# Bias rows and mask products in place of bias tables, scan products on four array quadrants, and three engines in written order

## The chip, the cores and the metric

The kernel runs on one core of one Trainium2 chip. The metric is the device time of one execution in microseconds; less is better. The profile gives busy times of TensorE (PE, and PEld for its weight loads), VectorE (DVE), ScalarE (ACT), GpSimd (POOL) and the queue of SyncE (SP), which issues all the DMAs of this program.

## The reference, cut to what matters

One layer over 2048 latent tokens (a grid of 32 rows by 64 columns) with 256 context tokens ahead of them. One input projection feeds two branches: neighbourhood attention and a gated delta rule in both directions; both are gated, projected, merged and projected again.

```python
# neighbourhood attention, per grid row r: 8 rows x 16 columns of keys around each query, plus all context keys
s_win = einsum('bqhd,bywhd->bhqyw', q_r, k_band) + bias      # bias: learned, by row and column distance
s_win = where(col_in, s_win, -inf)                           # only the query's own 16 columns
s_ctx = einsum('bqhd,bchd->bhqc', q_r, kc)
pr = softmax(concatenate([s_win, s_ctx]))                    # one softmax over both
o_na = pr_win @ v_band + pr_ctx @ vc
# delta rule, per chunk of 64 tokens and direction, state S (64 x 64 per head)
v_new = u_i - w_i @ S
o_i = qd_i @ S + qk_i @ v_new
S = S * gt_i + kd_i.T @ v_new
# merge
y = sigmoid(g_na) * ((o_na * silu(z_na)) @ w_o_na) + sigmoid(g_dn) * ((rmsnorm(o_dn) * silu(z_dn)) @ w_o_dn)
out = x + gate * (y @ w_out)
```

## The kernel before

All matrix products that need more than one pass of reduced precision are written as three products of a high and a low part (names ending in H and L, or `hi` and `lo`); the small ones of the scan, of the transposes and of the values run in plain float32, which TensorE takes in two passes.

The stages, in order of time. **Setup** (0 to 126 us): norms and transposes of the inputs. **Delta-rule projections**: the blocks for q, k and v with short convolution, then `kk_tile`, which forms the k k^T and q k^T products of each chunk, beside gate projections. **Attention projections** (`na_pair`, 920 to 1271 us): 52 tiles of 256 tokens in six series (v, k, v, k, q, q), each tile 48 matmuls on L729; tiles of k and q are normalised: squares on ACT (L691), a scale on DVE (L693), a power on POOL (L694), a multiplication on ACT (L697), then, two tiles later, a transpose on PE (L707), an eviction on ACT into the single buffer `nhi` (L710) and a store. DVE runs the triangular solves (`solve`, L580 and L582) beside it. **Bias tables** (`table_load`, `table`, L760 to L787): for each of the 8 heads, 8 DMAs bring skewed rows of the padded bias from `d_rp` into `trr` (16 partitions each), and 9 additions on POOL (L782) add them to masks read from `k_mk`; the results go to `d_tab`. The scheduler places this work beside the later attention projections and the gate projections, from 1091 us on. **Last gate units and the scan over the context** (1393 to 1451 us).

**Attention and scan** (1451 to 2009 us). A loop of 32 units: 2 groups of 4 heads (`hg`), 4 groups of 8 grid rows (`rg`), 4 groups of 16 columns (`cg`). A unit has 128 queries and a band of 12, 15 or 16 rows by 24 or 32 columns of keys, so 288 to 512 window keys, and 256 context keys. It treats its 4 heads as two pairs `pr`. For each pair: `scores` (three products for each head on L1079, then one DVE operation, L1089, that adds the bias table and takes the row maximum), `scores_ctx` (the same against context keys, L1079; the maximum on L1096, its negative `nm` on L1098, and four exponentials on ACT, L1101 and L1104), `turn` (transposes of the window probabilities, L1112, copied by DVE and ACT, L1114), `turn_ctx` (L1121, L1123), `values` (L1132, L1136), and for the unit `sums_inv` (L1140 to L1144) and `finish` (L1149 to L1153). The queries of two units come by one DMA and are split by `split_later` into `qh` (ACT, L977) and `ql` (POOL, L978). The tables come from `d_tab`: those of the inner row groups into `tmid`, the others into `tedge`.

Between these calls, `pump(chain, n)` advances the scan, one step of both directions for each unit: `times_state` twice (L882: k and q against the state, DVE on L884 and L887), `cT` (L898), its copy `cw` on ACT (L900), `ckd` (L905, state update on L906), `cA` (L912, output `co` on L914), and on POOL the state's decay (L894) and, in the second half, the sum of the two directions (L892). Direction 0 lies on partitions 0 to 63, direction 1 on 64 to 127; each product is 64 x 64 on the quadrant of the array where its rows and columns have the same half. From unit 17 on a unit also holds `dn_out` of the step before: a square on ACT (L928), its sum on DVE (L930, L931), a power on POOL (L933), a multiplication on DVE (L934), four transposes on PE (L938), one DVE operation (L939) and a store.

PE runs the loop in the order in which it is written (`manual_schedule` on L994); the order on DVE, ACT, POOL and SP is that of the program's scheduler, which goes by its own costs. Every engine then executes its own list strictly in that order. **Output** (2009 to 2389 us): the branch projections (L1356) and the final one (L1367).

## Time and profile before

| | us |
|---|---|
| device time, median of 3 runs | 2390.23 (2381.87 to 2395.80) |
| profiled execution, its own time | 2390.53 |
| span from its first to its last instruction | 2388.7 |
| PE busy / DVE / ACT / POOL | 2198.5 / 1500.3 / 849.5 / 943.1 |

Busy times are shares of the whole span; how much an engine is waited for differs by stage, so the sections below go by stretches of time. A matmul's end is modelled, so PE reads as busy a little beyond its last column. The granted clock of TensorE is shown as a share of 2.4 GHz; its mean was 0.973.

### The profile page before, as it was taken

To read this page: it belongs to the slowest core of one execution; us is meant where nothing else is said; L and a number is where in the kernel's file an instruction comes from. 1 tells how busy PE (TensorE), PEld (TensorE's weight loads), DVE (VectorE), ACT (ScalarE), POOL (GpSimd) and SP (SyncE) were. 2 spreads that over 40 slices of the span, in tenths; PEclk is the share of its full clock that TensorE was granted. 3 is DMA by queue.
4 is the path that set the end of the run, shared out by engine and by line. 5 is a ranking of instruction groups with operands and counts; after the bars stand their busy time and mean duration, and the time that the engine had idled before them with its cause. 6 is when DMAs were issued, how large, how long until landed. Compare 5 with 4: busy or idle time off the path is not lost. (4 is left out here: it accounts for less than half of the span.)

```text
span 2388.7 us, 47331 instructions
## 1 busy us (share of the span) xinstructions
PE 2198.5 (92%) x18359; PEld 1842.5 (77%) x18359; DVE 1500.3 (63%) x2410; ACT 849.5 (36%) x2624; POOL 943.1 (39%) x784
## 2 busy tenths in 40 slices
PE   6999999998989999999889997999888988999999
PEld 2778777876767778998887876777666766889988
DVE  3736877469959969859669813666566766222222
ACT  4524344344333332434554112444334444211110
POOL 2514777654423102316758410211133325543442
PEclk8999999999999999999999998999999999999999
DMA  7323444665574153254676667877877776444342
GB/s 267 105 74 76 115 126 121 158 154 141 146 190 124 55 127 89 60 135 132 179 189 187 167 182 214 224 188 205 210 200 186 186 194 195 139 118 128 108 116 91
DMA packets 461592, 358.17 MB, mean 150 GB/s; under 512 B 203253, under 2 KB 386697, under 8 KB 460809
## 3 DMA queue, kind: packets, MB, share of 16 engines
q1 hardware_dynamic: 461368, 355.16, 55.6%
q8 instruction: 144, 2.36, 0.4%
q14 instruction: 80, 0.66, 0.1%
HBM read 231.71 MB, written 119.67 MB: 147 GB/s over the span
## 5 line engine op out<-in xcount | busy, mean ns | idle before, releaser
L179 PE MATMUL pd<-hT,slots 128*128 128x512 f32 (+1 forms) x3360 | 812.5, 396 | 1.8 <-ACT hT L319 1.7
L179 PEld LDWEIGHTS pd<-hT,slots 128*128 128x128 f32 x3360 | 619.0, 191 | 146.8 <-issue 3.8
L580 DVE TENSOR_TENSOR tmp<-Xs 128x236 f32<-128x236 f32 (+43 forms) x310 | 313.0, 1010 | 38.3 <-DMA Xs<-d_X 26.1
L582 DVE TENSOR_TENSOR Xs<-Xs,tmp 128x236 f32<-128x236 f32 (+43 forms) x310 | 324.2, 1046 | 8.6
L125 POOL TENSOR_TENSOR slots<-w_raw,slots 128x512 fp32r<-128x512 f32 (+1 forms) x76 | 117.3, 1544 | 343.2 <-ACT slots L124 336.5
L729 PE MATMUL pd<-slots,hT 128*128 128x256 f32 x1248 | 162.2, 290 | 0.0
L729 PE MATMUL pd<-wide,hT 128*128 128x256 f32 x1248 | 159.5, 290 | 2.4 <-ACT wide L124 1.3
L729 PEld LDWEIGHTS pd<-wide,hT 128*128 128x128 f32 x1248 | 156.4, 197 | 3.2 <-ACT wide L124 1.8
L729 PEld LDWEIGHTS pd<-slots,hT 128*128 128x128 f32 x1248 | 156.9, 193 | 0.0
L1101 ACT ACTIVATE pr<-pr,nm 128x288 f32<-128x288 f32 (+3 forms) x128 | 77.9, 609 | 161.3 <-DVE nm L1098 161.3
L894 POOL TENSOR_TENSOR sd<-sd,gts 128x512 f32<-128x512 f32 x36 | 37.6, 1043 | 214.2 <-PE pc L882 200.2
L1357 DVE SCALAR_TENSOR_TENSOR gt<-gt,pu 128x256 f32<-128x256 f32 x120 | 46.2, 418 | 120.4 <-DMA gt<-d_g 62.5
L782 POOL TENSOR_TENSOR tmk<-trr,tmk 128x288 f32<-128x288 f32 (+3 forms) x72 | 99.4, 1397 | 37.9 <-DMA tmk<-in_k_mk_dram 33.2
L484 DVE SCALAR_TENSOR_TENSOR y<-raw,vT,y 128x512 f32<-128x512 f32 (+1 forms) x112 | 95.1, 860 | 24.3 <-ACT raw L472 20.4
L1371 DVE SCALAR_TENSOR_TENSOR ckd<-pf,gate 128x512 f32<-128x512 f32 x32 | 22.0, 691 | 122.2 <-PE pf L1367 111.7
L1356 PE MATMUL pu<-ckq,OS 128*128 128x256 f32 x512 | 95.2, 284 | 1.5 <-DVE gt L1357 1.4
L205 ACT ACTIVATE zt<-pd 128x512 f32<-128x512 f32 x73 | 43.3, 593 | 145.9 <-PE pd L179 80.2
L694 POOL TENSOR_TENSOR nrn<-nss,nhalf 128x8 f32<-128x8 f32 x34 | 72.6, 2136 | 54.6 <-DVE nss L693 54.3
L1358 POOL TENSOR_TENSOR gt<-gt 128x256 f32<-128x256 f32 x60 | 44.1, 735 | 123.8 <-DVE gt L1357 111.5
L124 ACT CAST slots<-w_raw 128x512 fp32r<-128x512 f32 (+1 forms) x76 | 46.6, 613 | 129.9 <-DMA w_raw<-in_w_in_dram 107.7
L1359 ACT CAST yh<-gt 128x256 fp32r<-128x256 f32 x60 | 24.3, 406 | 187.4 <-POOL gt L1358 187.3
L1112 PE MATMUL pt<-ident,pr 128*128 128x128 f32 (+2 forms) x416 | 66.2, 286 | 23.5 <-ACT pr L1101 22.3
(298 smaller groups left out, 4614.8 us busy)
## 6 DMA issues: line engine op xcount, KB each, us to landing
w_raw<-in_w_in_dram SPq DMA_DIRECT2D x92, 256.0 KB
ckq<-d_kq SPq DMA_DIRECT2D x64, 256.0 KB
gt<-d_g SPq DMA_DIRECT2D x60, 256.0 KB
d_g<-zt SPq DMA_DIRECT2D x41, 256.0 KB
d_X<-X SPq DMA_DIRECT2D x72, 128.0 KB
Xs<-d_X SPq DMA_DIRECT2D x18, 512.0 KB
cv<-d_v SPq DMA_DIRECT2D x72, 128.0 KB
cT<-d_T SPq DMA_DIRECT2D x72, 128.0 KB
```

What stands on the lines that cost most here:

```text
L124: S.copy(hi[:, j:j + 4, 0:n], wr)
L125: G.tensor_tensor(out=lo[:, j:j + 4, 0:n], in0=wr, in1=hi[:, j:j + 4, 0:n].bitcast(F32), op=ALU.subtract)
L179: PE.matmul(ps[0:n, 0:m], a[:, k, 0:n], h_part(g, z, k), start=k == 0 and i == 0, stop=k == KB - 1 and i == 2)
L484: V.scalar_tensor_tensor(out=y[:, 0:m], in0=raw[:, o + j - 1:o + j - 1 + m], scalar=tap(j), in1=y[:, 0:m], op0=ALU.mult, op1=ALU.add)
L580: V.tensor_tensor(out=tv, in0=X[r, piv, cols].unsqueeze(1).to_broadcast([8 * n, m, w]), in1=X[r, rows, piv].unsqueeze(2).to_broadcast([8 * ...
L582: V.tensor_tensor(out=X[r, rows, cols], in0=X[r, rows, cols], in1=tv, op=ALU.add)
L694: G.tensor_tensor(out=rn, in0=ss, in1=nhalf, op=ALU.pow)
L729: PE.matmul(ps[:, 256 * i:256 * i + 256], h[:, 256 * j + P * i:256 * j + P * i + P], w[:, :, part, k, :], start=k == 0 and n == 0, stop=k ...
L782: G.tensor_tensor(out=mv, in0=rr[:, k0:k0 + nr, w0:w0 + n], in1=mv, op=ALU.add)
L1101: S.activation(e[:, 0:nk], e[:, 0:nk], AF.Exp, bias=nm[:, u:u + 1], accum_out=self.sums[:, hh, 0:1])
L1112: PE.transpose(ptw[0:kb, b, :], self.et[u][:, kb * b:kb * b + kb], ident)
L1356: PE.matmul(ps, a, r[:, k, :], start=k == 0 and n == 0, stop=k == 3 and n == 2)
```

## The change

It has three parts.

1. **Bias and masks.** The tables, their DMAs and their POOL additions are gone. `load_bias` brings the skewed bias rows of 4 heads straight into an SBUF tile `bias` (two of them), with the same 8 DMAs for each head; for the first group all 32 are issued ahead of the first query load, for the second group four in each of units 6 to 13. The mask is added on PE: two more products for each head and pair in `scores`, ahead of the three others and into the same PSUM region, with a 64-row one-hot matrix of the query's row (then of its column) as stationary operand and a row (column) mask, repeated by a stride of zero, as moving one. DVE then adds the bias from a strided view of the tile.
2. **Scan.** `times_state` becomes one block: for each head, the products with k and with q follow each other, the latter into the other half of the partitions, so four quadrants take part. In the same way `ckd` and `cA` are interleaved. Buffers in DRAM that hold tokens of the scan's output swap halves, and a second copy of the decay factors with halves swapped (`egw`) is loaded.
3. **Order.** DVE, ACT and POOL too run the 32 units in the order in which they are written, and that order is changed: five advances of the scan for each unit in place of seven, `scores_ctx` ahead of `values`, both `turn_ctx` copies on ACT, `dn_out` spread over the second, third and fourth advance, `sums_inv` after the second `turn`.

```diff
-    def table(h):
-        ...
-                SP.dma_start(out=mk, in_=k_mk[:, ty, o:o + nr * n])
-                ...
-                G.tensor_tensor(out=mv, in0=rr[:, k0:k0 + nr, w0:w0 + n], in1=mv, op=ALU.add)
-                SP.dma_start(out=d_tab[:, ty, h, o:o + nr * n], in_=mk)
...
-            def times_state(z):
-                ps = pc.tile([P, H, C], F32, name="pc")
-                for h in range(H):
+            pss = [pc.tile([P, H, C], F32, name="pc") for _ in range(2 if main else 1)]
+            for h in range(H):
+                for z, ps in enumerate(pss):
                     for d in range(2):
-                        PE.matmul(ps[half[d], h, :], ld["ckq"][half[d], ho(h), z, :], sd[half[d], h, :], start=True, stop=True)
+                        PE.matmul(ps[half[d ^ z], h, :], ld["ckq"][half[d], ho(h), z, :], sd[half[d], h, :], start=True, stop=True)
...
             for h in range(H):
                 for d in range(2):
                     PE.matmul(p4[half[d], h, :], ld["ckd"][half[d], h, :], w[half[d], h, :], start=True, stop=True)
+                for d in range(2 if main else 0):
+                    PE.matmul(p3[half[1 - d], h, :], ld["cA"][half[d], ho(h), :], w[half[d], h, :], start=True, stop=True)
...
+        def load_bias(hg):
+            z = ap.tile([P, 4, 16, 47], F32, name="bias", bufs=2)
+            for h in range(4):
+                for qr in range(8):
+                    if qr % 4 == 0:
+                        yield z
+                    o = ((4 * hg + h) * 23 + 7 - qr) * 47
+                    behind(SP.dma_start(out=z[16 * qr:16 * qr + 16, h].rearrange("q k w -> q (k w)"), in_=skew[:, o:o + 16 * 47]))
...
+                for i, (a, b) in enumerate(more):
+                    for u, r in enumerate(halves):
+                        PE.matmul(out(u), a[r], b[r], start=i == 0, stop=False)
...
-                    V.tensor_tensor_reduce(self.e[u][:, 0:nk], pws[u][:, 0:nk], self.tab[pr][:, u, 0:nk], 1.0, -3.0e38, ALU.add, ALU.max, self.mx[:, u, 0:1])
+                    V.tensor_tensor_reduce(rc(self.e[u][:, 0:nk]), rc(pws[u][:, 0:nk]), biases[self.hg][:, 2 * pr + u, k0:k0 + self.nr, w0:w0 + w], 1.0, -3.0e38, ALU.add, ALU.max, self.mx[:, u, 0:1])
...
-        mid_load = load_mid(0)
-        mids = {0: next(mid_load)}
+        bias_load = load_bias(0)
+        biases = {0: next(bias_load)}
+        for _ in bias_load:
+            pass
+        mkraw = ap_("fwr").rearrange("p a b -> p (a b)")[:, 0:432]
+        SP.dma_start(out=mkraw, in_=k_mk)
...
         load_q(0)()
...
+        order_all = tc.manual_schedule(engines={mybir.EngineType.DVE, mybir.EngineType.Activation, mybir.EngineType.Pool})
+        order_all.__enter__()
```

The loop's body after the change (the diff of it is long):

```python
pump(chain, 1); un.turn(); un.scores(1)
pump(chain, 1); un.turn_ctx(); un.scores_ctx(1)
pump(chain, 1); un.values(0)
pump(chain, 1); splits; un.turn(); un.sums_inv(); nu.scores(0)      # nu: the next unit
pump(chain, 1); un.turn_ctx(); nu.scores_ctx(0); un.values(1); un.finish()
```

**SP, just ahead of the first unit.** `fwr<-d_nq` is the load of the first queries, `tmid` a table, `d_g<-zd` the store of the last gate unit. Before:

```order
L863 DMA cv<-d_v 64x512
L864 DMA cT<-d_T 64x512
L863 DMA cv<-d_v 64x512
L864 DMA cT<-d_T 64x512
L974 DMA fwr<-d_nq 128x2x256
L992 DMA tmid<-d_tab 128x1232
L211 DMA d_g<-zd 128x512
```

and now, with line numbers of the changed program (`bias<-d_rp` is one of the 32 loads of bias rows):

```order
L834 DMA cv<-d_v 64x512
L835 DMA cT<-d_T 64x512
L975 DMA bias<-d_rp 16x752 x2
L213 DMA d_g<-zd 128x512
L975 DMA bias<-d_rp 16x752 x30
L1221 DMA fwr<-in_k_mk_dram 128x432
L951 DMA fwr<-d_nq 128x2x256
```

The first query load has moved behind 32 loads of bias rows, the masks and a store.

**PE, a unit with `dn_out`** (15-row band, 360 keys), from the last transposes of the unit before on. Before:

```order
L1149 MATMUL po<-ident,rb 128x128 x2
L882 MATMUL pc<-sd,ckq 64x64 x16
L1112 MATMUL pt<-ident,pr 120x128 x6
L882 MATMUL pc<-sd,ckq 64x64 x16
L1121 MATMUL pt<-ident,pr 128x128 x4
L1079 MATMUL pw<-KH,qh 128x360 x2
L1079 MATMUL pw<-KL,qh 128x360 x2
L1079 MATMUL pw<-KH,ql 128x360 x2
L898 MATMUL pc<-cv,cT 64x64 x16
```

and now (`mkr` are the mask products, L913 the transposes of `dn_out`):

```order
L853 MATMUL pc<-sd,ckq 64x64 x32
L1091 MATMUL pt<-ident,pr 120x128 x6
L1051 MATMUL pw<-mkr 128x360 x4
L1054 MATMUL pw<-KH,qh 128x360 x2
L1054 MATMUL pw<-KL,qh 128x360 x2
L1054 MATMUL pw<-KH,ql 128x360 x2
L1100 MATMUL pt<-ident,pr 128x128 x4
L1054 MATMUL pw<-KHc,qh 128x256 x2
L1054 MATMUL pw<-KLc,qh 128x256 x2
L1054 MATMUL pw<-KHc,ql 128x256 x2
L871 MATMUL pc<-cv,cT 64x64 x16
L1111 MATMUL po<-pT,vt 64x128 x6
```

The two blocks of 16 scan products have become one of 32, four mask products stand ahead of the scores, and the context transposes and scores now stand ahead of `cT`.

**DVE, the same kind of unit**, where `dn_out` has its sum (`so`) and its multiplication (`co<-co,ro`). Before, at the unit's end:

```order
L1089 ISA mx 128x1
L930 TENSOR_REDUCE so<-ob 128x8
L931 TENSOR_SCALAR so<-so 128x8
L1096 TENSOR_REDUCE mx<-pw 128x1 x2
L1152 TENSOR_TENSOR azt<-po,azt 128x16x16
L1098 TENSOR_REDUCE nm<-mx 128x2
L1153 TENSOR_TENSOR azt<-po,azt 128x16x16
L934 TENSOR_TENSOR co<-co,ro 128x512
```

and now, in mid-unit (`pr,mx<-pw,bias` is the addition of the bias):

```order
L857 TENSOR_TENSOR cr<-pc,egw 128x512
L1075 TENSOR_REDUCE mx<-pw 128x1 x2
L1077 TENSOR_REDUCE nm<-mx 128x2
L905 TENSOR_REDUCE so<-ob 128x8
L906 TENSOR_SCALAR so<-so 128x8
L909 TENSOR_TENSOR co<-co,ro 128x512
L914 SCALAR_TENSOR_TENSOR zd<-pc,vT,zd 128x512
L1093 COPY pT<-pt 128x384
L1119 TENSOR_TENSOR ri<-sums 128x4
```

The multiplication by `ro`, which POOL makes from `so`, follows `so` directly, and the copy `pT` of the second `turn` stands behind both it and `zd`.

## Rows read from the trace of the kernel before

**Rows 1.** Windows by stage: length, busy time and instructions by engine, clock, DMA.

```profile
1091.00:1290.00 199.00, 172.41 (x1299) 165.37 (x1298) 150.71 (x157) 107.13 (x629) 143.97 (x90) 0.95 0.67 178
1451.00:1480.80 29.80, 17.01 (x257) 13.91 (x257) 10.32 (x30) 6.83 (x21) 2.71 (x3) 0.77 0.79 208
1480.80:1744.40 263.60, 235.81 (x3986) 189.34 (x3984) 167.44 (x449) 112.74 (x339) 47.38 (x52) 0.97 0.80 208
1744.40:2008.60 264.20, 232.09 (x3791) 184.99 (x3790) 186.26 (x470) 118.79 (x339) 91.89 (x87) 0.97 0.73 190
```

**Rows 2.** Windows, of L729 alone: length, PE and PEld busy, clock, DMA.

```profile
992.20:1035.10 42.90, 42.90 (x338) 41.54 (x337) 1.00 0.59 125
1101.60:1265.00 163.40, 136.82 (x1011) 131.69 (x1010) 0.95 0.69 183
```

**Rows 3.** Chain of waits from 1091 to 1290 us: total, times, longest.

```profile
ACT nx L697 <- POOL nrn L694: 51.1, 21, 4.2
ACT nhi L710 <- DMA d_nq<-nhi: 14.5, 5, 6.1
```

**Rows 4.** Groups by line, POOL, 1091 to 1290 us: busy, mean ns, idle before.

```profile
L782 POOL TENSOR_TENSOR tmk<-trr,tmk 128x288 f32<-128x288 f32 (+3 forms) x51 | 68.7, 1366 | 23.3 <-DMA tmk<-in_k_mk_dram 19.3 <-issue 1.9 <-DMA d_nk<-nhi 1.8
```

**Rows 5.** Timeline of SP around 1154 us: start, duration, four issues merged.

```profile
1153.76 1.81 SPq L768 DMA_DIRECT2D trr<-d_rp  x4
```

**Rows 6.** Timeline ahead of the first unit: start, duration, idle time before in brackets.

```profile
1455.43 0.37 SPq L974 DMA_DIRECT2D fwr<-d_nq  x1
...
1461.59 0.62 ACT L977 CAST qh<-fwr 128x512 fp32r<-128x512 f32 x1 [11.28 <-DMA fwr<-d_nq]
...
1462.26 0.61 PE L1079 MATMUL pw<-KH,qh 64*128 64x288 f32 x2 [11.51 <-ACT qh L977]
```

**Rows 7.** Timeline of PE within one unit.

```profile
1645.06 1.15 PE L882 MATMUL pc<-sd,ckq 64*64 64x64 f32 x32
...
1647.78 1.15 PE L882 MATMUL pc<-sd,ckq 64*64 64x64 f32 x32
1648.86 0.66 PE L1121 MATMUL pt<-ident,pr 128*128 128x128 f32 x4
...
1649.72 0.32 PE L1079 MATMUL pw<-KL,qh 64*128 64x360 f32 x2
1649.88 0.33 PE L1079 MATMUL pw<-KH,ql 64*128 64x360 f32 x2
```

**Rows 8.** Windows of 0.20 us in one `kk_tile`, L628 alone (passes under way).

```profile
626.95:627.15 0.20, 0.20 (x8) 0.16 (x4) 1.00 0.26 62
626.40:626.60 0.20, 0.20 (x16) 0.20 (x10) 1.00 1.15 267
```

**Rows 9.** Windows: unit 12, and unit 17.

```profile
1659.90:1674.00 14.10, 13.65 (x249) 11.11 (x247) 10.13 (x28) 6.11 (x20) 1.44 (x2) 1.00 0.87 233
1744.40:1767.60 23.20, 17.90 (x252) 14.28 (x251) 12.49 (x32) 7.99 (x23) 5.77 (x6) 0.85 0.85 206
```

**Rows 10.** Chain of waits, 1480 to 2009 us.

```profile
DVE pr L1089 <- DMA tedge<-d_tab: 17.2, 8, 4.4
...
PE pw L1079 <- POOL ql L978: 11.6, 11, 2.0
...
PE pw L1079 <- DVE mx L1089: 10.2, 8, 3.6
```

**Rows 11.** Groups by line, DVE, ACT and POOL, 1760 to 2011 us.

```profile
L1096 DVE TENSOR_REDUCE mx<-pw 128x1 f32<-128x256 f32 x56 | 21.1, 418 | 8.8 <-PE pw L1079 8.5
L884 DVE TENSOR_TENSOR cr<-pc,egs 128x512 f32<-128x512 f32 x28 | 19.2, 687 | 8.7 <-PE pc L882 8.3
L1089 DVE CUSTOM_DVE_ANT_0 pr<-pw,tmid 128x360 f32<-128x360 f32 (+1 forms) x32 | 18.4, 608 | 4.5 <-PE pw L1079 4.5
L1114 DVE COPY pT<-pt 120x384 f32<-120x384 f32 (+3 forms) x29 | 17.0, 586 | 0.8 <-PE pt L1112 0.8
...
L1101 ACT ACTIVATE pr<-pr,nm 128x360 f32<-128x360 f32 (+3 forms) x57 | 35.0, 615 | 63.5 <-DVE nm L1098 63.5
L1104 ACT ACTIVATE pr<-pw,nm 128x256 f32<-128x256 f32 x58 | 26.3, 455 | 0.0
...
L933 POOL TENSOR_TENSOR ro<-so,nh 128x8 f32<-128x8 f32 x15 | 24.7, 1647 | 30.9 <-DVE so L931 30.6
L892 POOL TENSOR_TENSOR cr<-cr,OS 128x512 f32<-128x512 f32 x14 | 18.7, 1337 | 0.0
L894 POOL TENSOR_TENSOR sd<-sd,gts 128x512 f32<-128x512 f32 x14 | 14.6, 1043 | 54.9 <-PE pc L882 52.5 <-DMA ckd<-d_kd 2.5
L978 POOL TENSOR_TENSOR ql<-fwr,qh 128x512 fp32r<-128x512 f32 x7 | 8.9, 1270 | 0.0
```

More of the change, by code (lines that the diff above doesn't have):

```diff
@@ L956, in scan @@
                 yield
-                yield from step
-                yield
+                next(step, None)
                 yield
@@ L1071, in __init__, with products @@
                 self.po = None
-            def products(self, pr, keys, out):
+            def products(self, pr, keys, out, more=()):
                 q0 = P * (self.n % 2)
+                halves = [slice(64 * u, 64 * u + 64) for u in range(2)]
+                for i, (a, b) in enumerate(more):
+                    for u, r in enumerate(halves):
+                        PE.matmul(out(u), a[r], b[r], start=i == 0, stop=False)
                 for i, (a, b) in enumerate(((0, 0), (0, 1), (1, 0))):
-                    for u in range(2):
-                        r = slice(64 * u, 64 * u + 64)
-                        PE.matmul(out(u), self.qs[a][r, pr, q0:q0 + P], keys(b)[r], start=i == 0, stop=i == 2)
+                    for u, r in enumerate(halves):
+                        PE.matmul(out(u), self.qs[a][r, pr, q0:q0 + P], keys(b)[r], start=i == 0 and not more, stop=i == 2)
             def scores(self, pr):
@@ L1280, in body @@
             un.turn()
-            nu = Unit(n + 1, *ahead) if ahead else None
-            pump(chain, 1)
-            un.turn_ctx(1)
+            un.sums_inv()
+            nu = Unit(n + 1, ahead) if n < 31 else None
             if nu:
@@ L1287, in body @@
                 pump(gprod, 1000)
-            un.values(1)
+            pump(chain, 1)
+            un.turn_ctx()
             if nu:
                 nu.scores_ctx(0)
+            un.values(1)
             un.finish()
-            pump(chain, 1)
             un = nu
```

141 lines of the change are left out of this document (57 added, 84 removed).

## The prediction

> **What bounds the kernel now.** I first cut the span into stages by windows of busy time, then asked in each which wait ends last. Three stages hold everything that the change touches: the stretch in which the bias tables are made, the start of the attention, and the 32 units.
>
> In 1091 to 1290 us PE is busy for 172.4 of 199.0 us, with the DMA engines at 0.67 and the clock at 0.95 [rows 1]. Seven tiles of L729 without table work beside them took 42.9 us, 6.13 each; 21 tiles with it took 163.4 us, 7.78 each [rows 2]. So the stretch is 21 x 1.65 = 34.7 us longer than at the earlier pace. The chain of waits says where: ACT's normalising multiplication waits 51.1 us in all for POOL's `nrn`, and its eviction 14.5 us for the store that empties `nhi` [rows 3]. POOL meanwhile makes 51 table additions of 1.37 us [rows 4], and `nrn` queues behind them. Behind it, beside the gate units, PE is busy for 102.1 of 103.0 us [rows 1]: no room, nothing to win.
>
> At the start of the attention PE stands idle for 11.5 us, since the first queries' load was issued at 1455.43 and `qh` could be made only at 1461.59 [rows 6]. The stretch ran at clock 0.77 [rows 1].
>
> In the units PE is the bound: 235.8 of 263.6 us in the first half, 232.1 of 264.2 in the second, while DVE has 167 and 186, POOL 113 and 119 [rows 1]. What PE lacks goes to single waits: `ql` from POOL, 11.6 us, and the maximum of DVE, 10.2 us, which itself waits 17.2 us for table loads [rows 10]. Two units show the spread: unit 12 takes 14.1 us, 13.65 of it PE work; unit 17, the first with `dn_out`, 23.2 us at clock 0.85 with one wait for DVE's maximum of up to 3.6 us [rows 9, 10].
>
> **The tables.** With the POOL additions and their DMAs gone, POOL has `nrn` as its first duty again. All of the 34.7 us would return if the tables were the whole difference, none if these series (queries, with stores to `nhi` [rows 3]) were slower by themselves. The 14.5 us behind `nhi`'s stores need not be the tables' doing, but the table DMAs share their queue. I take three quarters, **-26**, bounds 0 and -35.
>
> **The start.** Thirty of the 32 bias loads, the masks and the last gate store now stand ahead of the first query load. Four such loads took 1.81 us on SP [rows 5], so 30 take 13.6, and the mask load one more of 0.4; two table loads at about 0.5 each go. All of it stands on the path: PE has nothing before the queries come [rows 6]. **+13**; bounds 0 (if SP gets to these loads well before) and +16 (all 32, the masks and the store's own time).
>
> **PE's work in a unit.** Removed: a block of 16 scan products is 32 passes in 1.15 us [rows 7], of which about 0.2 is the modelled tail, so 0.94. What a block takes with four quadrants is read from `kk_tile`, where windows of equal length hold 8 passes with two quadrants in use and 16 with four, at full clock in both [rows 8]: a pass costs its quadrant 0.05 us (0.20 x 2 / 8 and 0.20 x 4 / 16) either way. Two blocks of 32 passes become one that lasts as long as either, and this happens twice in a unit: 2 x 0.94 = -1.88. Added: mask products. Two products over 360 keys (both heads of a pair, on opposite row halves) start 0.16 us apart [rows 7]; there are two such steps in a `scores` call and two calls: 4 x 0.16 = +0.66. A moving operand with a stride of zero isn't in the trace; were it twice as slow, another 0.66 x 32 = 21 us would go, and at no cost at all 21 come back. I take it as an ordinary one, since only its address is special. Net -1.2 a unit, -39 over 32, if waits stayed as they are.
>
> The Trainium skill speaks against the four quadrants: its page "TensorEngine Tiling (Array Packing)", section "Restrictions and Gotchas", says that different row tiles can't access the same PSUM bank at the same time. By it the four would run two at a time, and the saving of 60 us (32 x 1.88) would be nil. The trace disagrees: L882 writes both row halves into one buffer, and its 32 passes took 1.15 us where one after the other they would need 32 x 0.05 = 1.6 [rows 7, 8].
>
> **Waits in a unit.** The order on the other engines is now written, so I walked one unit by hand, from the end of the block of 32. PE needs 0.8 (second `turn`), 1.0 (scores with masks), 0.55 (`turn_ctx`, L1121's 0.66 less its tail [rows 7]), 0.6 (context scores), 1.0 (`cT`) and 1.45 (values): 5.4 to the next `turn`. DVE needs in its order `cr` and `cv` 0.69 each, `pT` 0.58, two bias operations of 0.61, `cr` again, two maxima of 0.42, `nm` 0.15: 4.9 with the operations' accumulator reads; then ACT's exponential 0.61 and its sum 0.19 [rows 11]: 5.9. So `turn` waits about 0.5; `cw`, behind four exponentials, costs 0.1. Unit 12's 13.65 [rows 9] becomes 13.65 - 1.88 + 0.66 = 12.4; with the waits **13.0** for an even unit. In an odd unit the split of the next queries stands in the written order behind `cw`: `qh` 0.61 on ACT [rows 6], then `ql` 1.27 on POOL [rows 11], and the next unit's scores wait some 2.2: **15.1**. Six of the key splits (1.27 on POOL [rows 11]) in the first 16 units add 7.6, and four units with 512 keys about 1 each. Units 1 to 16: 8 x 13.0 + 8 x 15.1 + 7.6 + 4 = 236 against 263.6 [rows 1]: **-27**. The table loads' waits on DVE (17.2 [rows 10]) are in that difference.
>
> From unit 17 on `dn_out` comes in. Four transposes add 0.55 to PE. Its chain is: DVE done with `nm` at 5.1, `so` 0.68 and its scaling 0.27 on DVE, POOL busy with the sum of directions (1.34) and the decay (1.04) until 6.6, `ro` 1.65 [rows 11], so 8.25, `co` 0.69, so 8.95. PE, in its written order, stands at the transposes at 5.4: it waits 3.55, in place of the 0.5 above. 12.95 + 3.55 = **16.5**; 15 x 16.5 + 4 = 251.5 against 264.2: -13. Such waits lower the clock: unit 17 lost (1 - 0.85) x 23.2 = 3.5 us beside a wait of 3.6 [rows 9, 10]. I take half of that in about a quarter of the 15 units, +6 (bounds 0 and 52): **-7**. Queued behind `co` on DVE are `zd` and the copy `pT` of the next `turn`, so the wait is late for `values` too, but PE has stood still meanwhile.
>
> Queue of SP: by the changed program's order about 19 DMAs a unit, at 0.45 [rows 5] are 9 us, with four bias loads 11, less than a unit. It hides behind PE, and would cost only if units fell below that.
>
> **Sum.** 2390.5 - 26 + 13 - 27 - 7 = **2343 us**, against the profiled execution's 2390.53 (span 2388.7 and 1.8 around it), which stands 0.3 above the median of the runs, 2390.23.
>
> **Rivals.**
> 1. *The `dn_out` wait costs more.* For it: every wait of 3.5 us is as long as unit 17's [rows 10]. Against it: in the second half as a whole the clock was 0.97 [rows 1]. At half of 3.5 us in each of the 15 units, 26 in place of 6, and a little in the odd units of the first half: 2343 + 27 = 2370. Chance 0.14.
> 2. *The table stage doesn't recover.* `nrn` and `nhi`'s store then set the pace by themselves, as rows 3 leave possible; against it, POOL's 68.7 us of additions [rows 4] fall away. 2343 + 26 = 2369. Chance 0.10.
> 3. *Quadrants run two at a time.* +60: 2403, slower. Rows 8 speak against it. Chance 0.05. It is what the rule of the Trainium skill's tiling page would make of it.
> 4. *The clock, slower side.* Fixed orders give PE one wait of over 2 us in 23 of the 32 units (8 odd ones, 15 with `dn_out`), always at the same place. If each costs what unit 17's did, 23 x 3.5 - 6 = +74: 2417. It decides from 2.85 us a wait on ((47 + 12 + 6) / 23). Against it: unit 17's clock also carries two other idle times. Chance 0.08. The Trainium skill, "TensorE: Matmul & The Clock Gate", section "Why this matters for your kernels", warns of idle gaps between bursts as what returns the engine to half rate; by it rival 4 is the natural course, and unit 17's 0.85 agrees, though the half's 0.97 doesn't.
> 5. *Most waits vanish,* if POOL gets to `ro` before the sum and the decay, or the squares come a step earlier than I read: 15 x 1.9 less, 2315. Chance 0.05.
>
> **How the numbers follow.** My forecast has 0.58, with its own range 2325 to 2365 (tables 0 to -35 around -26, start, stride). Measured runs of the kernel spread from 2381.87 to 2395.80, so 0.5%, 12 us, is what can be told from no change. Rivals 3 and 4 lie above 2388 (0.13), half of rival 5 and a little of the forecast below 2308: the range 2308 to 2388 leaves out less than 0.2. Faster by over 0.5%: nearly all of the forecast, rival 5, and some six sevenths of rivals 1 and 2, 0.81. Slower by over 0.5%: rival 3 and most of rival 4, 0.11. Between: 0.08.
>
> **What would show it.** Tables: 21 tiles at about 6.5 us, and ACT's wait for `nrn` mostly gone. Start: the query load issued some 13 us later after the last gate unit, PE idle for about 24 us. Scan: the block of 64 passes on one line in 1.15 us, not 2. Units: even ones of 13, odd ones of 15 with a wait for `ql`; from 17 on one wait of about 3.5 us at the transposes of `dn_out`, ended by DVE's `co`, that by POOL's `ro`. I am wrong if the block lasts 2 us, if mean clock in the units falls below 0.93, or if a wait that I left at nothing (`cw` behind the exponentials, the copy `pT` behind `co`) shows up with over 1 us in each unit.

## The result and the profile after

The changed kernel takes 2373.2 us (median of 12 runs, 2369.3 to 2380.88), the kernel before 2390.4 on the same chip: a ratio of 0.9929 (95% interval 0.9918 to 0.9939). The gain is real, 17 us, but little more than a third of the 47 that were forecast. The span of the profiled execution is 2371.4 us against 2388.7, so the two traces differ by 17.3 us too, and the stretches of both can be set against each other:

| stretch (from PE's first or last instructions) | before | after | difference | forecast |
|---|---|---|---|---|
| up to the attention projections | 920.0 | 923.1 | +3.1 | 0 |
| attention projections (L729, now L731) | 351.9 | 325.0 | -26.9 | -26 |
| from there to the scan over the context | 121.5 | 115.3 | -6.2 | 0 |
| scan over the context to the end of the first unit | 87.4 | 97.6 | +10.2 | +13 |
| units 1 to 16 | 263.6 | 250.4 | -13.2 | -27 |
| units 17 to 31 | 264.7 | 278.3 | +13.6 | -7 |
| output | 379.6 | 381.7 | +2.1 | 0 |

The two rows of the units hold the miss. Windows of the two halves of the units, of two units of the first half (one without and one with a split of the next queries) and of one with `dn_out`; columns as in [rows 1]:

```profile
1461.00:1711.40 250.40, 223.94 (x4114) 177.47 (x4113) 160.84 (x429) 121.10 (x354) 48.89 (x51) 0.92 0.75 198
1711.40:1989.30 277.90, 222.14 (x3909) 179.90 (x3907) 195.29 (x457) 127.68 (x355) 92.65 (x85) 0.88 0.65 167
...
1479.30:1491.70 12.40, 12.02 (x257) 9.87 (x255) 9.57 (x27) 6.78 (x22) 2.68 (x3) 1.00 0.80 206
1491.70:1509.80 18.10, 15.02 (x256) 11.96 (x254) 9.54 (x27) 8.46 (x26) 3.88 (x4) 0.81 0.67 178
1730.90:1750.40 19.50, 15.32 (x260) 12.78 (x258) 13.16 (x30) 8.15 (x24) 5.57 (x5) 0.82 0.70 170
```

The even unit takes 12.4 us at full clock. In the other two PE's work *grew* to 15 us with nearly the same products, because the granted clock fell to 0.81 and 0.82: for a part of these units TensorE had 1.2 GHz in place of 2.4. Over the halves it is 0.92 and 0.88 where both were 0.97 [rows 1]. The trace keeps when the clock was at half rate: for 41.0 us of the first half and 64.9 of the second, and PE was working in 37.8 and 55.7 of them. Work at half rate takes twice as long, so half of that, 18.9 and 27.9 us, is what the clock cost; in the kernel before it was 6.8 and 8.5. This fits the traces: with the cost taken off PE's busy time, the work of units 1 to 16 is the same in four runs that have the same products there, 205.0 us (changed kernel), 206.0 (late transposes), 206.6 (wait filled) and 204.6 (early splits), though their clocks and busy times differ.

PE's own waits in the units of the changed kernel (total, times, longest):

```profile
PE pc L913 <- DVE co L909: 53.6, 15, 5.1
PE pw L1054 <- ACT qh L954: 8.8, 8, 1.6
PE pw L1054 <- POOL ql L955: 8.8, 7, 2.1
PE po L1111 <- DMA vt<-d_nv: 3.2, 2, 1.9
```

They are the forecast ones: 53.6 us in 15 units are 3.57 each on average, and 17.6 in eight odd units 2.2 each. The chain through one unit with `dn_out` (start, us, what) shows where the long one comes from:

```profile
1735.40 0.61 DVE cr L857
...
1736.15 1.27 POOL cr L865
1737.42 1.00 POOL sd L867
...
1738.53 1.66 POOL ro L908
...
1740.21 1.78 DVE co L909
...
1742.03 1.11 PE pc L913 x4
```

The power `ro` stands behind the sum of the directions and the state's decay on POOL, and DVE's multiplication behind that. The average of 3.57 hides two kinds of unit: seven of the 15 waits are 2.9 to 3.0 us, six are 4.0 to 4.1, and the other two 3.6 and 5.1. In the first kind DVE's `co` takes 0.69 us, in the second 1.74 to 1.79; there POOL had begun its next split, into `KL` or `ql`, at most 0.07 us before (timelines of POOL and DVE in the unit of the chain, then of DVE in one of the first kind, with no split beside it):

```profile
1740.17 1.26 POOL L955 TENSOR_TENSOR KL<-fwr,KH 128x512 fp32r<-128x512 f32 x1
1740.21 1.77 DVE L909 TENSOR_TENSOR co<-co,ro 128x512 f32<-128x512 f32 x1 [1.76 <-POOL ro L908]
1777.60 0.69 DVE L909 TENSOR_TENSOR co<-co,ro 128x512 f32<-128x512 f32 x1 [1.76 <-POOL ro L908]
```

In two units `co` began first, by 0.2 us: there it took 0.69, and the split behind it 1.67 in place of 1.26. So here whichever of the two began second was held up by the other, and that is 1.1 us of the longer waits.

The scan's block is as forecast: 64 passes in the time in which before 32 took 1.15 us [rows 7] (timeline of PE, even unit):

```profile
1479.68 1.16 PE L853 MATMUL pc<-sd,ckq 64*64 64x64 f32 x64
1480.77 0.88 PE L1091 MATMUL pt<-ident,pr 128*128 128x128 f32 x6
1481.58 0.61 PE L1051 MATMUL pw<-mkr 64*128 64x384 f32 x4
1482.02 0.34 PE L1054 MATMUL pw<-KH,qh 64*128 64x384 f32 x2
```

The four mask products of a call take 0.44 us over 384 keys until the first score product starts, where two steps of ordinary ones take 0.36. The projections beside which the tables were made run at their old pace (L731 alone, columns as in [rows 2]):

```profile
992.20:1035.10 42.90, 42.90 (x337) 41.51 (x336) 1.00 0.53 112
1101.60:1240.00 138.40, 133.23 (x1021) 128.57 (x1020) 0.99 0.39 91
```

1021 products need 138.4 us, 1011 needed 163.4 [rows 2].

### The profile page after: what moved, and what is told of

It reads as the page before. It is cut to its first block, busy times and chain, and to the rows that moved or that the text cites. A ratio compares the mean times of both kernels' runs of the same rounds, so it can differ in the third digit from the quotient of the medians.

```text
span 2371.4 us, 47485 instructions
## 1 busy us (share of the span) xinstructions
PE 2162.9 (91%) x18615; PEld 1814.3 (77%) x18615; DVE 1468.9 (62%) x2378; ACT 868.3 (37%) x2657; POOL 844.4 (36%) x712
## 4 chain that ended last, share of the span: by engine, by line
PE 52%; DVE 18%; DMA 10%; POOL 8%; issue 7%; ACT 2%; SPq 2%; POOLq 0%; DVEq 0%; ACTq 0%
PE pd L181 19%; PE pf L1354 7%; PE pu L1343 7%; DVE Xs L584 6%; DVE tmp L582 6%; PE pd L731 5%; PE pw L1054 2%; PE pc L880 2%; PE pt L1091 1%; POOL rn L509 1%; PE pc L853 1%; POOL ro L908 1%; POOL xa L521 1%; PE po L1111 1%; PE pw L1051 1%
## 5 line engine op out<-in xcount | busy, mean ns | idle before, releaser
L582 DVE TENSOR_TENSOR tmp<-Xs 128x236 f32<-128x236 f32 (+43 forms) x310 | 302.5, 976 | 36.8 <-DMA Xs<-d_X 28.1
L584 DVE TENSOR_TENSOR Xs<-Xs,tmp 128x236 f32<-128x236 f32 (+43 forms) x310 | 305.6, 986 | 8.4
L731 PE MATMUL pd<-slots,hT 128*128 128x256 f32 x1248 | 160.4, 288 | 0.0
L731 PE MATMUL pd<-wide,hT 128*128 128x256 f32 x1248 | 156.4, 287 | 2.4 <-ACT wide L127 1.4
L731 PEld LDWEIGHTS pd<-wide,hT 128*128 128x128 f32 x1248 | 153.6, 193 | 3.3 <-ACT wide L127 1.8
L731 PEld LDWEIGHTS pd<-slots,hT 128*128 128x128 f32 x1248 | 155.2, 191 | 0.0
L1068 DVE CUSTOM_DVE_ANT_1 pr<-pw,bias 128x288 f32<-128x288 f32 (+3 forms) x128 | 66.3, 553 | 69.5 <-PE pw L1054 69.5
L1102 ACT COPY pTc<-pt 128x512 f32<-128x512 f32 x64 | 37.5, 586 | 137.9 <-PE pt L1100 137.9
```

The source lines that it names most:

```text
L582: V.tensor_tensor(out=tv, in0=X[r, piv, cols].unsqueeze(1).to_broadcast([8 * n, m, w]), in1=X[r, rows, piv].unsqueeze(2).to_broadcast([8 * ...
L584: V.tensor_tensor(out=X[r, rows, cols], in0=X[r, rows, cols], in1=tv, op=ALU.add)
L731: PE.matmul(ps[:, 256 * i:256 * i + 256], h[:, 256 * j + P * i:256 * j + P * i + P], w[:, :, part, k, :], start=k == 0 and n == 0, stop=k ...
L1068: V.tensor_tensor_reduce(rc(self.e[u][:, 0:nk]), rc(pws[u][:, 0:nk]), biases[self.hg][:, 2 * pr + u, k0:k0 + self.nr, w0:w0 + w], 1.0, -3. ...
```

## The experiments

The theory to test: the units lost their forecast gain to the clock, which falls around PE's two regular waits. The rivals: the units are bound by a chain (DVE, POOL) or by transfers, and waits and clock only show it. The 27.9, 18.9 and 6.8 us of the expectations are the clock's cost as counted above. Windows, waits and timelines are those of one execution of each version. The kernel before took 2392 to 2395 us on the chips of these runs, so the changed kernel would be at about 2377 there; ratios are to the kernel before.

| run | us | ratio (95% interval) |
|---|---|---|
| late transposes of `dn_out` | 2338.0 | 0.9766 (0.9749 to 0.9783) |
| wait filled with useless products | 2368.7 | 0.9894 (0.9865 to 0.9922) |
| early splits | 2383.8 | 0.9957 (0.9940 to 0.9974) |
| two quadrants at a time | 2406.9 | 1.0048 (1.0027 to 1.0068) |
| start reordered | 2377.7 | 0.9936 (0.9916 to 0.9956) |
| order left to the scheduler | 2371.8 | 0.9907 (0.9883 to 0.9931) |
| before, no additions on POOL | 2386.4 | 0.9963 (0.9948 to 0.9978) |
| late transposes, early splits, start | 2333.5 | 0.9748 (0.9722 to 0.9774) |
| the same, gate loads late | 2328.4 | 0.9720 (0.9691 to 0.9749) |
| the same three, SP in written order | 2357.1 | 0.9836 (0.9808 to 0.9865) |
| changed, additions back on POOL | 2401.3 | 1.0033 (1.0015 to 1.0051) |
| gate loads late, two more moves | 2330.0 | 0.9740 (0.9712 to 0.9769) |

**The transposes of `dn_out` later.**

```diff
+            yield
             V.tensor_tensor(out=oa, in0=oa, in1=ro.unsqueeze(2).to_broadcast([P, H, C]), op=ALU.mult)
...
                 next(dn, None)
-                yield
                 next(step, None)
                 yield
+                next(dn, None)
+                yield
...
             un.values(0)
-            pump(chain, 1)
...
                 nu.scores_ctx(0)
+            pump(chain, 1)
             un.values(1)
```

> The transposes of dn_out move from the fourth advance of the scan to a place behind the next unit's context scores, and the multiplication by ro goes behind the next unit's bias operations; nothing else changes. In the changed kernel PE waits 53.6 us in all at these transposes (15 times about 3.6 us), and the clock at half rate takes another 27.9 us of PE's working time in units 17 to 31. Theory A (these waits, and the clock that falls during each, are what the second half lost): the waits shrink to under 1 us each, most of the half-rate stretches go, 42 us of waiting and about 20 us of clock come back: about 2312 us. Theory B (DVE, busy for 195 of 278 us there, is the bound whatever the place of the transposes): PE waits as long at another tile, 2360 to 2373 us.

2338.0 us, 39 less than the changed kernel. PE's waits (units 17 to 31) and the windows of the two halves:

```profile
PE pw L1056 <- POOL ql L957: 6.6, 7, 1.6
PE pc L914 <- DVE sd L883: 5.6, 7, 1.2
PE pw L1056 <- ACT qh L956: 5.6, 7, 1.2
```

```profile
1462.50:1710.50 248.00, 220.02 (x4115) 173.66 (x4113) 159.14 (x427) 121.50 (x354) 48.73 (x51) 0.94 0.76 197
1710.50:1957.80 247.30, 221.24 (x3907) 172.37 (x3907) 193.44 (x460) 126.61 (x355) 90.50 (x86) 0.92 0.73 190
```

The wait of 53.6 us is 5.6; the second half is 31 us shorter, with the same work on DVE, so DVE was not the bound. Theory A holds for the waits, short of its number: the splits' wait, hidden behind the long one until now, appears in the odd units (12.2 us), and the clock comes back only to 0.92. PE is busy for as long as before (221.2 us for 222.1), so what came back here is idle time; the price of the clock isn't shown by this run but by the next.

**The wait filled.** Nothing gets shorter here; PE only has something to do.

```diff
             pt2 = pc.tile([P, 4, P], F32, name="pc")
+            for k in range(18):
+                PE.matmul(pt2[:, k % 4, :], ident, ident, start=True, stop=True)
```

> Eighteen products of the identity with itself are added ahead of the transposes of dn_out, into the PSUM tile that the transposes then overwrite; they need nothing that is late, last about 2.5 us and so fill the larger part of PE's wait of 3.6 us with useless work. No chain of the program gets shorter. Theory A (a wait costs its own length and then the clock): the clock stays at full rate in units 17 to 31, and most of the 27.9 us that half rate took there come back: about 2352 us. Theory B (the units are bound by the chain through DVE and POOL, and a slower PE only fills up waits that would be there anyway): no change, 2370 to 2376 us.

2368.7 us. First the unit with `dn_out` that is the last window of the changed kernel above; then units 17 to 30 together, here and in the changed kernel:

```profile
1733.80:1750.50 16.70, 16.70 (x296) 14.51 (x294) 12.98 (x30) 8.09 (x24) 5.59 (x5) 1.00 0.65 153
1716.80:1970.90 254.10, 244.33 (x4168) 209.25 (x4168) 180.90 (x429) 118.83 (x329) 85.74 (x80) 0.99 0.67 171
1711.80:1966.10 254.30, 205.10 (x3662) 167.88 (x3662) 182.36 (x429) 118.80 (x331) 86.07 (x80) 0.89 0.68 174
```

The same unit takes 16.7 us in place of 19.5, with more work on PE, at clock 1.00 in place of 0.82. In the five units whose wait was about 4 us and which don't wait for `vt` here, 1.4 to 2.8 us come back, with nothing in the chain made shorter (`co` takes 1.75 us or more there as before). Over the 14 units, though, nothing is left of it in this execution: 254.1 us for 254.3. The trace shows two reasons. The filling took longer than meant (36 passes, 4.3 us busy, in a unit), so that units whose wait was 2.9 us gained at most 0.5 us or grew, two of them because their clock had stayed at 1.00 without filling; and PE now waited 8.6 us for `vt`, of which below. The four runs lie between 2361.75 and 2375.54 us, and the profiled one is the slowest, so where the 9 us of the median come from isn't seen.

A pair that no edit touches gives the price of the clock by itself. Unit 1 has the same program and the same two waits in both kernels (1.32 and 1.44 us in the changed one, 1.33 and 1.44 in this one), but not the same clock; first the changed kernel, then this one:

```profile
1461.40:1479.70 18.30, 15.54 (x258) 12.12 (x258) 9.66 (x26) 8.64 (x26) 3.89 (x4) 0.81 0.70 192
1464.30:1480.10 15.80, 13.03 (x255) 10.08 (x254) 9.58 (x26) 7.92 (x24) 3.89 (x4) 1.00 0.74 187
```

The waits being equal, the 2.5 us between them are the clock's. The pair also sets a limit to theory A: a wait need not lower the clock. Of the eight odd units of the first half, four ran at 1.00 here and none in the changed kernel, with waits for the splits in all of them. What decides whether a given wait does, no run here shows.

**Early splits.**

```diff
             un.turn_ctx()
+            for f in splits:
+                f()
+            splits = ahead_splits
             un.scores_ctx(1)
```

(The same three lines go from ahead of the second `turn`.)

> The splits of the next queries and keys into high and low parts move from the fourth advance (behind the exponentials and cw on ACT) to the second (behind the copy of the context transposes, ahead of the exponentials). In the changed kernel's odd units PE waits 8.8 us for qh and 8.8 us for ql in all, and half rate takes 18.9 us of PE's working time in units 1 to 16 (6.8 in the kernel before). Theory A (these waits and the clock behind them are what the first half lost): 16 us of waiting and 12 us of clock come back, about 2346 us, and odd units take about as long as even ones. Theory B (the wait moves: ACT's exponentials come later by the split's 0.6 us to 1.2 us, and the next turn waits instead): 2362 us or more.

2383.8 us, slower by 6. Theory A fails, and of theory B only the number holds: the wait didn't move to the next `turn`. The waits for `qh` and `ql` are gone, and the first units run at 12.4 us; but PE now waits for `vt`:

```profile
1462.30:1711.10 248.80, 219.00 (x4115) 174.09 (x4113) 156.39 (x427) 122.08 (x354) 47.13 (x51) 0.92 0.77 196
1462.30:1474.70 12.40, 12.40 (x257) 10.12 (x255) 9.69 (x26) 8.01 (x24) 3.93 (x4) 1.00 0.83 220
```

```profile
PE po L1111 <- DMA vt<-d_nv: 24.9, 14, 2.5
```

The first half stays at 249 us. SP's timeline ahead of and beside the unit that began at 1598.1 shows why `vt` is late:

```profile
1593.95 1.14 SPq L1142 DMA_DIRECT2D oa<-in_mod_w_dram  x1
1595.13 0.43 SPq L975 DMA_DIRECT2D bias<-d_rp  x1
1597.07 1.24 SPq L975 DMA_DIRECT2D bias<-d_rp  x3
1598.78 0.72 SPq L951 DMA_DIRECT2D fwr<-d_nk  x1
1599.60 2.29 SPq L1024 DMA_DIRECT2D vt<-d_nv  x4
```

This unit's own `vt` is issued 1.5 us after its start, behind a gate load and four bias loads. The issues of these four took 0.3 to 0.4 us each, as in the kernel before; but SP stood still for 1.5 us between the first and the second. The reason can be read off the issues in the traces of all versions: the program gives its DMAs eight semaphores in turn, so that an issue waits until the DMA eight places before it has landed (here a load of `azt`, issued at 1589.34 and landed at 1597.05). In the second half the splits stand ahead of `ro` on POOL, and the wait at the transposes grew to 60 us.

**Two quadrants at a time.**

```diff
-            for h in range(H):
-                for z, ps in enumerate(pss):
+            for z, ps in enumerate(pss):
+                for h in range(H):
...
+            for h in range(H):
                 for d in range(2 if main else 0):
```

> The products of the scan are issued as in the kernel before, the block with k ahead of the block with q, and ckd ahead of cA, so that only two quadrants are in use at a time; buffers, order of the engines and everything else stay as changed. Each of the two places takes 0.94 us longer on PE in each unit. Theory A (the quadrants' gain is real where PE is the bound, and lost where PE waits for DVE anyway): even units of the first half 1.9 us longer, odd ones 1.3, those with dn_out 0.9: about 40 us in all, 2413 us. Rival 1 (the gain went into waits everywhere): 2373 to 2385. Rival 2 (the gain counts in full in each unit): 2433.

2406.9 us, 29 more. The block of 64 passes (timeline of PE) takes 0.75 us longer, not 0.94:

```profile
1482.93 1.91 PE L853 MATMUL pc<-sd,ckq 64*64 64x64 f32 x64
```

```profile
1463.90:1721.80 257.90, 235.06 (x4115) 192.53 (x4113) 168.02 (x428) 120.86 (x354) 46.80 (x51) 0.97 0.72 189
1721.80:2027.20 305.40, 250.51 (x3909) 207.75 (x3907) 199.62 (x460) 127.99 (x355) 92.64 (x85) 0.87 0.59 155
```

So the quadrants' gain is real and counted, but the other way round than theory A had it: 7.5 us in the first half and 27 in the second. In units 1 to 16 PE has 22 us more work, counted at full rate; but the clock is 0.97 there and cost 7.8 us in place of 18.9, and PE waits nowhere for `vt`. Why the clock is higher isn't shown: the splits are waited for as long as in the changed kernel, 18.5 us for 17.6. In the second half the block stands ahead of both PE's way to the transposes and the chain to `ro`; the wait stays (53.5 us for 53.6), and the longer block counts in full.

**The start.** Masks and queries loaded first, the bias of four heads by one DMA for each row of queries:

```diff
-            for h in range(4):
-                for qr in range(8):
+            for qr in range(8):
+                yield z
+                for h, m in ((0, 4),) if hg == 0 else ((0, 3), (3, 1)):
```

> The masks and the first queries are loaded ahead of the bias rows, and the bias rows of four heads come by 8 DMAs (first group) and 16 DMAs (second group) in place of 32, with the same bytes. In the changed kernel the stretch from the first product of the scan over the context to the first scores takes 80.3 us, 68.9 in the kernel before. Theory A (the 32 issues on SP ahead of the query load are the start's 11 us): that stretch falls to 67 to 70 us and the kernel to about 2361 us; where PE waits for vt in unit 14 (3.2 us), with SP's queue late by then, that wait goes too. Theory B (DVE waits for the bias rows themselves, 1.5 MB that must land, whoever is issued first): the stretch stays at 76 or more, 2370 to 2374 us.

2377.7 us: no change. The first products come 12.6 us earlier, 67.5 us after the scan's first, but then the wait is DVE's (timeline of DVE):

```profile
1442.63 0.46 DVE L1068 CUSTOM_DVE_ANT_1 pr<-pw,bias 128x288 f32<-128x288 f32 x1 [21.35 <-DMA ckd<-d_kd]
```

In the changed kernel that operation starts at 1446.47; it gains 3.8 us, not 12.6. The DMA named isn't read by it. What it waits for are the bias rows: the last of their eight DMAs, issued at 1433.13, landed at 1442.50. By the stretch to the first products theory A was right, by the time of the kernel theory B: the issues were not the whole of it, the rows have to land.

**Order left to the scheduler** (the four lines with `order_all` left out).

> As changed, but DVE, ACT and POOL are ordered by the scheduler again, as in the kernel before, with PE's written order unchanged. Theory A (the place of the transposes in PE's written order makes the wait, so another order on the other engines can move it but not remove it): PE still waits for co from unit 17 on and for ql in odd units, 2360 to 2385 us. Theory B (the written order of DVE, ACT and POOL is what loses the time): about 2345 us, waits at the transposes below 2 us. Theory C (the written order is itself a gain): 2390 us or more.

2371.8 us; its interval overlaps that of the changed kernel, so the written order of DVE, ACT and POOL is worth nothing that these runs can tell. Theory A's number holds; but PE doesn't wait for `co`, as theory A had it. The wait sits elsewhere (units, PE):

```profile
PE pw L1054 <- DVE mx L1068: 27.1, 20, 3.4
PE pt L1100 <- DVE pT L1093: 22.4, 15, 3.5
PE pw L1054 <- POOL ql L955: 15.6, 11, 2.4
```

**The tables from both sides.** The kernel before without its additions:

```diff
-                G.tensor_tensor(out=mv, in0=rr[:, k0:k0 + nr, w0:w0 + n], in1=mv, op=ALU.add)
```

> The kernel before, with the 51 additions on POOL that make the bias tables left out; their DMAs stay, and the masks alone go to the tables, so the bias is missing from the result. The changed kernel's attention projections are 27 us shorter than before's. Theory A (nrn queues behind the additions on POOL): most of that comes back here too, 2362 to 2370 us, and the chain of waits shows nrn at under 25 us. Theory B (the tables' DMAs delay the stores of nhi and the loads of weights): under 10 us come back, 2380 or more.

and the changed kernel with additions but no DMAs of tables:

```diff
+                G.tensor_tensor(out=mks[j % 3][:, 0:n], in0=mks[j % 3][:, 0:n], in1=mks[j % 3][:, 0:n], op=ALU.add)
...
-        na_pair(*pairs[i], places[i], na_ahead[i])
+        na_pair(*pairs[i], places[i], na_ahead[i], lambda: pump(tables, 1))
```

> The changed kernel with the 72 additions that the tables took on POOL put back at their places, on zeros in SBUF that nothing reads, without any of the tables' DMAs. Theory A (additions ahead of nrn on POOL made the attention projections of the kernel before slow): their 325 us become 340 or more, and the kernel 2388 us or more. Theory B (the tables' DMAs did it): 325 to 330 us, 2371 to 2378 us.

By its number theory B holds in the first run and theory A in the second. Either part keeps the projections slow without the other: 349.9 us without the additions, 354.9 with additions alone, against 351.9 before and 325.0 after. Without the additions, the product line alone and the waits of the stretch:

```profile
1101.60:1265.00 163.40, 135.37 (x1023) 130.79 (x1022) 0.94 0.81 217
```

```profile
ACT nhi L710 <- DMA d_nq<-nhi: 23.2, 7, 10.8
ACT nx L697 <- POOL nrn L694: 17.9, 12, 2.0
ACT nhi L710 <- DMA d_nk<-nhi: 17.9, 5, 4.3
```

The wait for `nrn` falls from 51.1 [rows 3] to 17.9 us, but that for `nhi`'s stores rises from 14.5 to 41.1, since the tables' DMAs run at once where they had waited for POOL (DMA share 0.81 against 0.69 [rows 2]). With the additions alone the DMA share is 0.33 and `nrn` holds the pace:

```profile
ACT nx L699 <- POOL nrn L696: 23.3, 15, 3.5
...
ACT zt L699 <- POOL nrn L696: 16.4, 3, 9.1
```

So two limits lay on top of each other, and the change took away both. Neither run holds the other part as it was, though. With the additions gone, 42 MB moved from 1091 to 1290 us where the kernel before moved 35 MB; with the DMAs gone, all 72 additions ran there where before 51 did [rows 4]. That either would hold the stage back in its old dose isn't shown.

**All three together, and what then bounds the units.** Late transposes, early splits and the start in one:

> Transposes of dn_out late, the splits of queries and keys early, and the start with fewer and later bias loads, all three together. With early splits alone the loads of vt became late (the last one was issued 1.3 to 5 us ahead of its use in units 8 to 14, against 8 to 14 us in the changed kernel), since SP's queue ran behind the shorter units. Theory A (SP's queue runs behind for the number of its issues, and 16 fewer bias loads in units 6 to 13 free it): vt is waited for less than 10 us in all, the gains add up: 2303 us to 2318 us. Theory B (SP or the DMA engines bound units of 12.4 us whatever the bias loads): vt is waited for 20 us and more, 2325 us to 2345 us.

2333.5 us, not told apart from the late transposes alone, as theory B had it. The loads of `vt` are waited for 38.6 us, 30.1 of them in units 1 to 16. Two runs asked what makes them late. The gate's loads moved:

```diff
-            pump(gprod, int(n < 17))
+            pump(gprod, int(n > 13))
```

(The gate's two loads also share one buffer name now.)

> As the three together (late transposes, early splits, fewer bias loads), but the 16 loads of 256 KB for the output gate, one in each of units 0 to 16, with the operation on DVE that uses each, come in units 14 to 30. The three together took 2333.5 us, with about 30 us of waiting for vt in units 4 to 14, where the DMAs moved some 200 GB/s. Theory A (what the first half's transfers carry bounds it): 2.8 MB less in units 4 to 14 is 8 per cent of their 34 MB, vt's waits fall by half, 2312 to 2322 us. Theory B (it is the order of SP's list that makes vt late, not the load): the waits stay, 2330 us or more.

and SP in written order:

```diff
-        order_all = tc.manual_schedule(engines={mybir.EngineType.DVE, mybir.EngineType.Activation, mybir.EngineType.Pool})
+        order_all = tc.manual_schedule(engines={mybir.EngineType.DVE, mybir.EngineType.Activation, mybir.EngineType.Pool, mybir.EngineType.SP})
```

(Besides, `behind`, which holds some DMAs in program order, does nothing in the 32 units.)

> As the three together, but SP too issues the DMAs of the 32 units in the order in which they are written: the loads for the next unit first (vt among them), then the scan's, then the stores. Theory A (the scheduler's list has vt behind stores that wait for a unit's last results): vt is issued a unit ahead, its waits fall below 8 us in all, 2305 to 2315 us. Theory B (transfers bound the first half): another load is late in vt's place, the units 1 to 16 stay at 245 us or more, 2325 us or more.

Windows of the two halves of the units with the gate's loads late:

```profile
1455.40:1691.10 235.70, 211.31 (x4115) 169.47 (x4113) 150.59 (x413) 121.83 (x354) 46.45 (x51) 0.95 0.77 194
1691.10:1940.90 249.80, 218.01 (x3909) 171.34 (x3909) 203.89 (x474) 127.42 (x355) 89.76 (x86) 0.94 0.79 201
```

The first half falls from 257.7 to 235.7 us, the second grows from 240.6 to 249.8. PE waits for `vt` for 17.3 us of the first, not quite the half that theory A asks for. In the whole, 2328.4 us, the interval overlaps with that of the three together, and the number lies outside both theories: by time alone it is inconclusive. With SP in written order `vt` comes early and another load is late instead:

```profile
PE pc L853 <- DMA ckq<-d_kq: 62.0, 30, 7.3
```

So theory A of the SP run fails and its theory B holds. What both runs suggest, and don't prove, is that the transfers bound the first half once PE's own waits are gone. The eight semaphores say how. In units 1 to 16 of the three together, 79 of the 296 issues began just when the DMA eight before them had landed, and 64 of the 82 us that SP stood still ended so; in written order it is 88 of 296 and 70 of 83. A DMA took about 6 us from issue to landing there (median), in the changed kernel 5.0. So the number of DMAs in a unit and the time that each takes to land both count; a version with more of them under way wasn't run.

**A last version**, on top of the gate's loads late: the sum of the directions behind `rb` on POOL, the state's addition ahead of the multiplication by `ro` on DVE (two statements moved).

> The version with the gate's loads late, in which PE still waits 1.0 to 1.4 us at the transposes of dn_out in odd units (for the state's addition on DVE, which stands behind the multiplication by ro), and once 5.3 us in unit 17 for rb, which stands on POOL behind the sum of directions that waits for a store to come back. Two moves: the sum of directions goes behind rb in POOL's order, and the state's addition ahead of the multiplication by ro on DVE. Theory A (such single places in the written order still cost, each with some clock): about 12 us less than the 2328 us of that version, 2310 to 2320 us. Theory B (the transfers set the pace of the second half too by now): another wait for vt grows, 2325 us or more.

2330.0 us: no gain over the version it builds on, so theory A fails; theory B's number holds, but `vt` is waited for no longer than before (23.7 us for 25.0). One of the expected waits moved to the next scan block, `co` is waited for instead, and the waits for `vt` stay.

## Why the prediction was wrong

**The step that failed** is the one that prices the clock: "Such waits lower the clock [...] I take half of that in about a quarter of the 15 units, +6". The forecast builds its units from unit 12, which ran at full clock, and adds 6 us of clock in units 17 to 31 and none in units 1 to 16. Measured, half rate cost 27.9 and 18.9 us: 46.8 us where 6 were put. Without it the units took 250.0 and 231.5 us, for which the forecast has 251.5 and 236. So work and waits together were right within 5 us, and the 41 us of clock, less some 11 us by which these and the other stretches came out below their forecasts, are the 30 us by which the sum missed. The prediction's own sign of being wrong, a mean clock below 0.93, came true with 0.92 and 0.88.

Rival 1, "the `dn_out` wait costs more", had the mechanism and gave 2370 us, close to the 2373 measured. Its 26 us for the 15 units are near the 27.9 measured; the little that it has in the odd units of the first half, 7 of its 27, was 18.9. The chance of 0.14 that it got was the error. What spoke for it was there to be read: the one unit of before with such a wait ran at 0.85 [rows 9]. I set the second half's 0.97 [rows 1] against it; but in that half no other wait of PE was longer than 2.0 us (chain of waits of the kernel before, PE, 1744 to 2009 us: total, times, longest), and the change put one of 2.9 us or more into each of the 15 units.

```profile
PE pw L1079 <- DVE mx L1089: 5.6, 3, 3.6
PE pw L1079 <- POOL ql L978: 4.4, 4, 2.0
```

An average over units without the wait says nothing on units with it. Rival 4 went too far the other way: 46.8 us over 23 waits are 2.0 each, below the 2.85 from which it would decide.

That the long wait was forecast as 3.55 us and measured as 3.57 is luck. In the chain above, counted from the end of the scan's block as the prediction does, POOL was free at 6.0 us and not at 6.6, so `ro` ended at 7.75 and not at 8.25; and `co`, put at 0.69, took 0.69 in seven units and 1.74 to 1.79 in six. Waits of 2.9 and 4.1 us average to the forecast. The 7.6 us for the splits of keys in units 1 to 16 don't show either: no wait of PE is for one, and the forecast of 236 had that much room in it. In the walk through the unit, DVE's 4.9, 0.61 and 0.19 are 5.7, not 5.9.

The rule that the prediction took from the Trainium skill, "TensorE: Matmul & The Clock Gate", section "Why this matters for your kernels" (idle gaps between bursts return the engine to half rate), agrees with most of the trace: 0.81 and 0.82 in units with a wait of 3 and 4 us, 1.00 in the even unit, and 1.00 when the same wait was filled. Two units of the changed kernel with waits of 2.95 and 2.96 us stayed at 1.00 all the same. The Trainium skill's rule on PSUM banks ("TensorEngine Tiling (Array Packing)", section "Restrictions and Gotchas"), by which the four quadrants would take turns, doesn't agree: 64 passes over four quadrants take 1.16 us, over two 1.91.

**Right in size, wrong or incomplete in mechanism.** The tables: -26.9 for -26. The prediction laid them on `nrn` behind POOL's additions; when these were gone, the tables' DMAs held the stage back, and the other way round. Behind this stage it saw nothing to win; there 6.2 us went too, of PE's idle time and clock, down to the same 115.3 us in both of the runs on the tables. The start: +10.2 for +13. The prediction put all of it on the issues ahead of the query load; with that order mended, the bias rows' landing takes its place.

**Right.** The block of the scan (1.16 us), the even units (12.4 to 13.6 us for 13.0; one unit waited 3.2 us for `vt`), and the order of events at the transposes. The saving of four quadrants was 0.75 us a place, not 0.94, and the mask products a fifth dearer than ordinary ones; the even units took this in.

**Not foreseen.** The prediction held SP's list for hidden unless units fell below 11 us: it counted what the issues take, and not what each waits for the landing of the DMA eight before it. Once PE's waits were taken away, `vt` came late in units of 12.4 us already.

## What to carry to other kernels

Price an idle stretch of PE twice: its length, and the work after it at half rate, unit by unit and not by a stage's mean clock. In the units here, two regular waits of 71 us in all came with another 46.8 us for the clock. Look in the written order for what the waiting instruction's input queues behind on a slower engine, and try to move the consumer later before the producer earlier: the first gave 39 us here, with nothing else changed, the second cost 6, as other transfers came late. And before a gain is booked for taking one load off an engine, ask what holds the same wait up from another side: here, with POOL's additions gone, the DMAs kept the stage slow, and with the DMAs gone the additions did.

## What was not expected of the hardware

Filling PE's wait with useless products made a unit 2.8 us shorter (19.5 to 16.7). The same unit with the same waits took 18.3 us in one run and 15.8 in another, at clocks of 0.81 and 1.00. And DVE's multiplication `co` took 1.74 to 1.79 us in place of 0.69 where an operation of POOL had begun just before it.
